# Weights of a held group released at k = 5, 6, 7 in place of 1, 3, 5, and x tiles transposed 20 tiles after silu in place of 14

## Chip, cores and metric

One core of a Trainium2 chip runs the whole program. The metric is device time in microseconds, the median of several runs. TensorE is called PE here, VectorE DVE, ScalarE ACT, GpSimd POOL and SyncE SP.

## What is computed

Four transformer-like layers over a sequence of 512 tokens of width 1024, batch 1, in float32: two layers of a first block, then two of a second.

```python
def hybrid_layer(x, ...):                       # first block, twice
    h = rms_norm(x, attn_pre_gain)
    u = h @ w_in                                # queries, keys, values, gates of two attentions
    o_a = swa_sink_attention(qa, ka, va, attn_sinks)
    o_b = nsa_attention(qb_raw, qb_rot, kc, vc, ks, vs, kw, vw, gates)
    mixed = sigmoid(g_a) * (o_a @ w_branch_a) + sigmoid(g_b) * (o_b @ w_branch_b)
    x = x + rms_norm(mixed @ w_out, attn_post_gain)
    h = rms_norm(x, ffn_pre_gain)
    return x + rms_norm(conv_ffn(h, ffn_w_up, ffn_conv_w, ffn_conv_b, ffn_w_down), ffn_post_gain)

    # second block, twice
    proj = rms_norm_2(x, norm1_w[i]) @ w_in[i]  # z, xbc, dt, q, k, v
    xbc = silu(depthwise_conv_centered(xbc, conv_w[i], conv_b[i]))   # 7 taps
    y_ssm = rms_norm_2((ssd(xs, dt, bm, cm) both ways + d_skip * xs) * silu(z), ssm_norm_w[i])
    x = x + concat(y_ssm, windowed_gqa(q, k, v, sink, band_bias)) @ w_out[i]
    g, u = split(rms_norm_2(x, norm2_w[i]) @ w_up[i])
    x = x + (silu(conv(g)) * u) @ w_down[i]
```

## The kernel before

Activations stand transposed: a tile is 128 features by 512 tokens, and the width is eight such tiles. All dense products go through one stream of weights, `Stream` (`W`): 3680 tiles of 128 x 128, packed in the order of their use into 460 chunks of `CH` = 8 tiles. A product in float32 precision is three matmuls (`mm3`, lines 530 to 532): high weights by high activations, low weights by high, high by low. High and low parts are float32r tiles.

A chunk passes through three steps. `load` has SP fetch it into one of four buffers `wraw` (line 306). `conv` makes its two parts, in one of four buffers each. For most chunks ACT writes the negated weights, rounded to float32r, to `wl` (line 319), then POOL issues a DMA that adds the exact weights from DRAM onto them (line 320), which leaves the rounding error, and ACT writes the rounded weights to `wh` (line 324). For chunks in the middle of an FFN DVE makes `wl` by a subtraction instead (line 329). `release(c)` is the step that drives both: it loads up to chunk c + 7 and converts up to chunk c + 4, so the conversion goes into the buffers of chunk c. As a rule `W.next` calls it when the stream enters a new chunk. The program is scheduled by hand (`manual_schedule`): each engine works through its instructions in the order in which the Python code issues them, and a wait holds up all that is behind it on that engine.

`W.defer(n, fn)` runs `fn` when the stream has gone n weight tiles further; that is the clock by which small work is placed between the matmuls.

A seam joins two dense stages around an rms norm. The last tiles of the first stage are made in two halves of 256 tokens (`HA`, `HB`), so that the norm of the first half can run while the second is being multiplied. `halves` goes over the eight tiles; in each step DVE scales and adds (lines 1445, 1447), ACT and DVE make `h` and `hl` (`split`, lines 420 and 421), and for the second half ACT also squares `x` and issues a store of it, `xd` (line 1455). What is left of these steps is in a generator, `hs.rest`.

`dense_group` makes four output tiles at once over the eight input tiles. Where `hs.rest` is there it goes over its weights twice: a first round over k = 0 to 7 on the first half of the tokens and a second on the other half. After each k of either round it takes one step of `hs.rest`; the last `h` tile's step is issued after k = 4 of the second round. Its 32 weight tiles are four chunks, c0 to c0 + 3, which fill all the buffers; `W.holding` keeps `W.next` from releasing any, and the second round does it by hand. This branch runs four times: for `ffn_w_up` and for the next layer's `w_in` (or `w_in_2`), in both layers of the first block. The groups start at chunks 49, 115, 164 and 230. The norm's sum is taken three tiles after the group and `finish`, which evacuates the four accumulators, runs seven tiles after it.

In the second block `layer2` makes eight x tiles of the conv (`conv_evac` at names x0 to x7), with tiles of q between the first five. An evacuation multiplies by the norm; then ACT and POOL start the seven-tap sum, DVE adds the other five taps (line 1582), and seven tiles later ACT applies silu (line 1587). `then` is `x_tokens` (or `b_tokens` for B0 and B1): four PE transposes into `xtp` (line 1697) and four ACT copies to `xtok` (line 1699). After the eighth x tile the z tiles follow, and between them the backward states (`advance`, line 1783 and 1787), whose product is read at `yo` (line 1869). All tiles of 128 x 512 come from one pool of 66 slots.

Of the kernel before, what the change touches and what calls it, by code (L numbers as in the profile page):

```python
# [249 lines left out]
def trunk_kernel(ctx: ExitStack, tc: tile.TileContext, xT, positions, wts, cst_d, oh_d, rb_d, cw1_d,  # L250
# [14 lines left out]
    def big(name, dt=F32):  # L265
        return pools["t"].tile([128, T], dt, tag="t", name=name)
# [7 lines left out]
    def bank(name, hold=False):  # L274
        b = banks.pop(0)
        t = psum.tile([128, T], F32, tag=f"b{b}", name=name)
        if hold:
            held[id(t)] = (b, t)
        else:
            banks.append(b)  # L280
        return t

    def free(t):
        banks.append(held.pop(id(t))[0])
# [4 lines left out]
    class Stream:  # L289
# [56 lines left out]
        def next(self, key):  # L346
            self.due(self.t)
            c, i = divmod(self.t, CH)
            if i == 0 and not self.holding:
                self.release(c - 1)  # L350
            name, l, r, cols = PLAN[self.t]
            assert (name, l, r) == key[:3], (PLAN[self.t], key)
            self.t += 1
            h, lo = self.hl[c]
            s = slice(128 * i, 128 * i + 128)
            return h[:, s], lo[:, s]
# [15 lines left out]
    W = Stream()  # L372
# [88 lines left out]
    def rstd_a(sq, n, act=False):  # L461

        sq.sums(len(sq.p))
        ps = sq.stat
        v = small(4, "var")
        V.tensor_reduce(v, ps[:, 0:128 * len(sq.p)].rearrange("p (a j) -> p j a", j=128)[:, 0:4, :], AX.X, OP.add)
        free(ps)
        r4 = small(4, "rs")
        if act:
            A.activation(v, v, AF.Sqrt, bias=epst, scale=1.0 / n)  # L470
            V.reciprocal(r4, v)
            return r4
        t4 = small(4, "rt")
        V.tensor_scalar(v, v, 1.0 / n, EPS, op0=OP.mult, op1=OP.add)
        V.tensor_scalar(r4.bitcast(I32), v.bitcast(I32), -0.5, float(0x5F3759DF), op0=OP.mult, op1=OP.add)
        for _ in range(3):
            V.tensor_mul(t4, r4, r4)
            V.scalar_tensor_tensor(t4, t4, -0.5, v, op0=OP.mult, op1=OP.mult)
            V.scalar_tensor_tensor(r4, t4, 1.5, r4, op0=OP.add, op1=OP.mult)
        return r4  # L480
# [18 lines left out]
    def rstd_b(r4, name="R"):  # L499
        R = big(name)  # L500
        pb = spread(r4)
        V.tensor_copy(R, pb)
        free(pb)
        return R
# [4 lines left out]
    class Tiles(list):  # L509
# [6 lines left out]
        def then(self, f):  # L516

            if self.rest is None:
                f()
            else:  # L520
                self.due.append(f)
# [3 lines left out]
    def mm3(acc, w, x, first, last, cs=None):  # L525
        wh, wl = w
        xh, xl = x
        if cs is not None:
            acc, xh, xl = acc[:, cs], xh[:, cs], xl[:, cs]
        PE.matmul(acc, wh, xh, start=first, stop=False)  # L530
        PE.matmul(acc, wl, xh, start=False, stop=False)  # L531
        PE.matmul(acc, wh, xl, start=False, stop=last)  # L532
# [28 lines left out]
    def dense_group(keys, hs, evacs, sq, store, x=None, after=None):  # L561

        accs = [bank("acc", True) for _ in range(4)]
        n = KT
        r4 = []
        if hs.rest is None:
            for k in range(n):
                for acc in accs:  # L570
                    mm3(acc, W.next(keys(k)), hs[k], k == 0, k == n - 1)
                if x is not None and k < 4:
                    sq.add(x[2 * k])
                    sq.add(x[2 * k + 1])
            r4.append(rstd_a(sq, D))
        else:
            c0 = W.t // CH
            ws = {}
            for k in range(n):
                for a, acc in enumerate(accs):  # L580
                    ws[k, a] = W.next(keys(k))
                    W.holding = True
                    mm3(acc, ws[k, a], hs[k], k == 0, k == n - 1, HA)
                next(hs.rest, None)
            for k in range(n):
                for a, acc in enumerate(accs):
                    mm3(acc, ws.pop((k, a)), hs[k], k == 0, k == n - 1, HB)
                next(hs.rest, None)
                if k % 2 and k < n - 1:
                    W.release(c0 + k // 2)  # L590
            run(hs.rest)
            hs.rest = None
            W.holding = False
            for f in hs.due:
                f()
            W.defer(3, lambda: r4.append(rstd_a(sq, D)))

        def finish():
            store["R"] = rstd_b(r4[0])
            late = [ev(acc) for acc, ev in zip(accs, evacs)]  # L600
            for acc in accs:
                free(acc)
            for f in late:
                if f:
                    f()
            if after:
                after()
        W.defer(5 if r4 else 7, finish)

    def run(gen):  # L610
        for _ in gen:
            pass
# [236 lines left out]
    def layer1(l, x, hs, sq, gnext, side):  # L849
# [186 lines left out]
        def after():  # L1036
            W.drip(rt)
            cw[0], cw[1] = windows(st.pop("kcb")), windows(st.pop("vcb"))
            for nm in ("ka", "qa0"):
                sw[nm] = swap(st[nm])  # L1040

        dense_group(win, hs, [evac_r(nm) for nm in ("kcb", "vcb", "ka", "qa0")], sq, st, x, after)
        x = None
        for j in range(1, 4):
# [260 lines left out]
        def pair(i):  # L1305
            if l == 0 and i > 2:
                side.step(1)
            if i == 0:
                dense_group(key("ffn_w_up", l), hs, [conv(0, "a0"), conv(FT, "v0"), conv(1, "a1"),
                                                     conv(FT + 1, "v1")],  # L1310
                            sq3, st3, x)
                x.clear()
            elif i > 1:
                run(dense(key("ffn_w_up", l), hs, conv(i, f"a{i}")))
                run(dense(key("ffn_w_up", l), hs, conv(FT + i, f"v{i}")))
            later(i, gated)
# [235 lines left out]
    def layer2(l, x, hs, sq, gnext):  # L1552
# [13 lines left out]
        def conv_evac(idx, name, wait=1, then=None):  # L1566
            def f(acc):
                u = big("u")
                V.tensor_mul(u, acc, st["R"])

                def late():
                    c = big("c")
                    A.activation(c, u, AF.Identity, bias=cb[:, idx:idx + 1], scale=cw[:, 36 + idx:37 + idx])
                    t = big("ct")
                    A.activation(t, u, AF.Copy, scale=cw[:, idx:idx + 1])
                    G.tensor_add(c[:, 3:T], c[:, 3:T], t[:, 0:T - 3])  # L1576

                    def taps():
                        for k in (1, 2, 4, 5, 6):
                            d = k - 3  # L1580
                            lo, hi = max(0, -d), min(T, T - d)
                            V.scalar_tensor_tensor(c[:, lo:hi], u[:, lo + d:hi + d],  # L1582
                                                   cw[:, 12 * k + idx:12 * k + idx + 1], c[:, lo:hi], op0=OP.mult,
                                                   op1=OP.add)

                        def silu():
                            A.activation(c, c, AF.Silu)
                            st[name] = c
                            if then:
                                W.defer(14, lambda: then(c))  # L1590
                        W.defer(7, silu)
                    W.defer(wait, taps)
                return late
            return f

        def raw_evac(name, scale=None):
# [7 lines left out]
            return f  # L1604

        dense_group(win, hs, [conv_evac(m, nm, w, th) for m, nm, w, th in (
            (8, "B0", 5, lambda c: b_tokens(0, c)), (9, "B1", 21, lambda c: b_tokens(1, c)),
            (10, "C0", 37, None), (11, "C1", 53, None))], sq, st, None if l else x)
# [590 lines left out]
```

## Time and profile before

| | |
|---|---|
| Median of 3 timed runs | 3111.31 us (3110.29 to 3114.95) |
| Profiled execution, its own time | 3115.91 us |
| Its span, first to last instruction | 3114.1 us |
| Mean granted clock of PE | 0.989 |
| PE, DVE, ACT, POOL busy | 97%, 62%, 54%, 15% |
| HBM read, written | 402.45 MB, 21.10 MB |
| Mean of the DMA engines over the span | 140 GB/s |

Times in rows are microseconds from the span's start. A row of the timeline gives the start, the duration, the engine and the source line, the operation, the tiles written and read, and in brackets how long the engine had been idle before it and what ended that. Where an engine name has a q (SPq, ACTq), its queue only issued a DMA. The granted clock is 1.0 for 2.4 GHz and 0.5 for 1.2 GHz.

### The profile page before, as it was taken

To read this page: it belongs to the slowest core of one execution; us is meant where nothing else is said; L and a number is where in the kernel's file an instruction comes from. 1 tells how busy PE (TensorE), PEld (TensorE's weight loads), DVE (VectorE), ACT (ScalarE), POOL (GpSimd) and SP (SyncE) were. 2 spreads that over 40 slices of the span, in tenths; PEclk is the share of its full clock that TensorE was granted. 3 is DMA by queue.
4 is the path that set the end of the run, shared out by engine and by line. 5 is a ranking of instruction groups with operands and counts; after the bars stand their busy time and mean duration, and the time that the engine had idled before them with its cause. 6 is when DMAs were issued, how large, how long until landed. Compare 5 with 4: busy or idle time off the path is not lost.

```text
span 3114.1 us, 41037 instructions
## 1 busy us (share of the span) xinstructions
PE 3034.8 (97%) x15024; PEld 2523.0 (81%) x15024; DVE 1917.4 (62%) x3726; ACT 1670.8 (54%) x3014; POOL 482.4 (15%) x482
## 2 busy tenths in 40 slices
PE   9999999999999999999999989999999998999998
PEld 8778888888877888888876778888888676888887
DVE  7677477374677738737576686463546768646353
ACT  4568554343457855434467777432346777743232
POOL 1222200000222210000025422000002542200000
PEclk9999999999999999999999999999999999999999
DMA  7744759475764385333577745633357874563432
GB/s 234 175 109 92 187 139 136 107 118 163 197 169 109 83 202 137 107 95 112 144 174 212 184 106 118 164 108 121 98 157 165 216 183 96 122 166 102 128 96 68
DMA packets 143270, 435.68 MB, mean 140 GB/s; under 512 B 17083, under 2 KB 22459, under 8 KB 143068
## 3 DMA queue, kind: packets, MB, share of 16 engines
q1 hardware_dynamic: 106396, 309.83, 33.2%
q0 software_dynamic: 32064, 114.83, 21.7%
q10 hardware_dynamic: 4608, 8.39, 0.7%
q8 instruction: 119, 1.95, 0.3%
q14 instruction: 83, 0.68, 0.1%
HBM read 402.45 MB, written 21.10 MB: 136 GB/s over the span
## 4 chain that ended last, share of the span: by engine, by line
PE 76%; ACT 8%; issue 7%; DVE 6%; DMA 2%; POOL 2%; SPq 0%; ACTq 0%; DVEq 0%; POOLq 0%
PE acc L530 22%; PE acc L532 22%; PE acc L531 22%; PE ops L757 2%; PE pt L739 2%; ACT wl L319 1%; DMA wl<-in_wts 1%; ACT p L2126 1%; PE sp L712 1%; DVE c L1582 1%; PE sp L713 1%; DVE X L692 1%; ACT pth L745 1%; POOL c L1576 1%; ACT of L767 1%
## 5 line engine op out<-in xcount | busy, mean ns | idle before, releaser
L530 PE MATMUL acc<-h,wh 128*128 128x512 f32 (+1 forms) x2592 | 1014.3, 391 | 9.0 <-ACT h L420 4.6
L531 PE MATMUL acc<-h,wl 128*128 128x512 f32 (+1 forms) x2592 | 987.4, 381 | 4.0 <-DMA wl<-in_wts 3.9
L532 PE MATMUL acc<-hl,wh 128*128 128x512 f32 (+1 forms) x2592 | 987.8, 381 | 0.6 <-DVE hl L421 0.4
L530 PEld LDWEIGHTS acc<-h,wh 128*128 128x128 f32 x2592 | 491.1, 189 | 101.5 <-issue 8.0
L532 PEld LDWEIGHTS acc<-hl,wh 128*128 128x128 f32 x2592 | 490.1, 189 | 96.4 <-DVE hl L421 1.9
L531 PEld LDWEIGHTS acc<-h,wl 128*128 128x128 f32 x2592 | 491.3, 190 | 91.8 <-DMA wl<-in_wts 5.6
L324 ACT ACTIVATE wh<-wraw 128x1024 fp32r<-128x1024 f32 x408 | 427.5, 1049 | 240.9 <-PE acc L532 205.7
L320 POOL DMA_DIRECT2D wl<-in_wts x216 | 188.1, 871 | 1943.3 <-ACT wl L319 1397.7
L329 DVE TENSOR_TENSOR wl<-wraw,wh 128x1024 fp32r<-128x1024 f32 x244 | 296.9, 1219 | 92.3 <-ACT wh L324 84.6
L530 PE MATMUL acc<-ah,wh 128*128 128x512 f32 (+1 forms) x726 | 278.2, 383 | 0.0
L319 ACT ACTIVATE wl<-wraw 128x1024 fp32r<-128x1024 f32 x216 | 226.8, 1050 | 95.2 <-PE acc L531 84.4
L532 PE MATMUL acc<-al,wh 128*128 128x512 f32 (+1 forms) x726 | 277.8, 383 | 0.0
L531 PE MATMUL acc<-ah,wl 128*128 128x512 f32 (+1 forms) x726 | 277.7, 383 | 0.0
L1293 ACT ACTIVATE c<-u,prm 128x512 f32<-128x512 f32 x88 | 71.1, 817 | 203.4 <-DVE u L1289 203.4
L739 PE MATMUL pt<-cst,p 128*128 128x128 f32 x752 | 145.4, 281 | 17.7 <-DVE nm L2124 4.2
L531 PEld LDWEIGHTS acc<-ah,wl 128*128 128x128 f32 x726 | 136.5, 188 | 26.7
L532 PEld LDWEIGHTS acc<-al,wh 128*128 128x128 f32 x726 | 136.4, 188 | 26.7
L530 PEld LDWEIGHTS acc<-ah,wh 128*128 128x128 f32 x726 | 136.5, 188 | 26.4
L1151 ACT ACTIVATE p<-p,nm 128x128 f32<-128x128 f32 x192 | 102.1, 532 | 62.6 <-DVE nm L1149 59.8
L745 ACT ACTIVATE pth<-pt 128x256 fp32r<-128x256 f32 (+2 forms) x320 | 130.7, 411 | 7.5 <-PE pt L739 5.1
L739 PEld LDWEIGHTS pt<-cst,p 128*128 128x128 f32 x752 | 93.8, 142 | 44.8 <-ACT p L2126 12.1
L1582 DVE SCALAR_TENSOR_TENSOR c<-u,prm,c 128x510 f32<-128x510 f32 (+2 forms) x120 | 98.5, 821 | 40.9 <-POOL c L1576 37.5
(339 smaller groups left out, 4809.9 us busy)
## 6 DMA issues: line engine op xcount, KB each, us to landing
wraw<-in_wts SPq DMA_DIRECT2D x460, 512.0 KB, 5.0
wl<-in_wts POOLq DMA_DIRECT2D x216, 512.0 KB, 7.1
cum<-cum_d SPq DMA_DIRECT2D x64, 256.0 KB, 7.2
xd<-x ACTq DMA_DIRECT2D x32, 256.0 KB, 2.0
x<-xd SPq DMA_DIRECT2D x32, 256.0 KB, 6.6
bias<-bias_d SPq DMA_DIRECT2D x32, 192.0 KB, 2.4
x<-in_xT SPq DMA_DIRECT2D x16, 256.0 KB, 8.0
cw<-in_cw SPq DMA_DIRECT2D x16, 256.0 KB, 7.2
```

What stands on the lines that cost most here:

```text
L319: A.activation(lo, r, AF.Copy, scale=-1.0)
L320: G.dma_start(out=lo, in_=wts[c], accum_op=OP.add)
L324: A.activation(h, r, AF.Copy)
L329: V.tensor_sub(lo, r, h.bitcast(F32))
L530: PE.matmul(acc, wh, xh, start=first, stop=False)
L531: PE.matmul(acc, wl, xh, start=False, stop=False)
L532: PE.matmul(acc, wh, xl, start=False, stop=last)
L739: PE.transpose(pt[:, 128 * n:128 * n + 128], t[:, 128 * (kb - b0):128 * (kb - b0) + 128], ident)
L745: A.activation(th[:, 0:w], pt[:, 0:w], AF.Copy)
L1151: A.activation(p[:, 0:w], p[:, 0:w], AF.Exp, bias=nm[:, col:col + 1], scale=-1.0, accum_out=den[:, col:col + 1])
L1293: A.activation(c, u, AF.Identity, bias=cb[:, idx:idx + 1], scale=cw[:, 88 + idx:89 + idx])
L1582: V.scalar_tensor_tensor(c[:, lo:hi], u[:, lo + d:hi + d], cw[:, 12 * k + idx:12 * k + idx + 1], c[:, lo:hi], op0=OP.mult, op1=OP.add)
```

## The change

It has two parts. In `dense_group`'s second round the three hand-made releases, of chunks c0, c0 + 1 and c0 + 2, are made after k = 5, 6 and 7 in place of k = 1, 3 and 5. In `conv_evac` the transposes of a conv tile are deferred by 20 weight tiles after silu in place of 14; that holds for B0, B1 and the eight x tiles of both layers of the second block.

```diff
@@ -586,8 +586,8 @@
                 for a, acc in enumerate(accs):
                     mm3(acc, ws.pop((k, a)), hs[k], k == 0, k == n - 1, HB)
                 next(hs.rest, None)
-                if k % 2 and k < n - 1:
-                    W.release(c0 + k // 2)
+                if k >= n - 3:
+                    W.release(c0 + k - (n - 3))
             run(hs.rest)
             hs.rest = None
             W.holding = False
@@ -1587,7 +1587,7 @@
                             A.activation(c, c, AF.Silu)
                             st[name] = c
                             if then:
-                                W.defer(14, lambda: then(c))
+                                W.defer(20, lambda: then(c))
                         W.defer(7, silu)
                     W.defer(wait, taps)
                 return late
```

## Rows read from the trace of the kernel before

**Rows 1.** Head of the page: busy time of each engine.

```profile
PE 3034.8 (97%) x15024; PEld 2523.0 (81%) x15024; DVE 1917.4 (62%) x3726; ACT 1670.8 (54%) x3014; POOL 482.4 (15%) x482
```

**Rows 2.** PE's waits: what waited for what: us in total, times, longest.

```profile
PE acc L531 <- DMA wl<-in_wts: 3.9, 4, 1.4
PE hid L935 <- issue: 3.7, 2, 2.5
PE xtp L1697 <- ACT c L1587: 2.8, 1, 2.8
```

**Rows 3.** Windows (us; busy by engine; PEclk; DMA): first group's second round.

```profile
414.87:426.39 11.52, 11.52 (x98) 11.52 (x97) 8.13 (x19) 10.85 (x17) 2.38 (x3) 1.00 0.80 225
```

**Rows 4.** Timeline of ACT, first group's second round.

```profile
415.31 0.51 ACT L420 ACTIVATE h<-x,prm 128x256 fp32r<-128x256 f32 x1 [0.21 <-DVE x L1447]
...
416.56 0.51 ACT L420 ACTIVATE h<-x,prm 128x256 fp32r<-128x256 f32 x1 [0.21 <-DVE x L1447]
...
417.83 1.06 ACT L319 ACTIVATE wl<-wraw 128x1024 fp32r<-128x1024 f32 x1 [0.24 <-PE acc L531]
...
423.48 0.50 ACT L420 ACTIVATE h<-x,prm 128x256 fp32r<-128x256 f32 x1
...
424.40 1.04 ACT L319 ACTIVATE wl<-wraw 128x1024 fp32r<-128x1024 f32 x1
```

**Rows 5.** Timeline of POOL, then of PE, around the first group's end.

```profile
419.19 0.86 POOL L320 DMA_DIRECT2D wl<-in_wts  x1 [14.86 <-ACT wl L319]
...
426.67 0.50 PE L531 MATMUL acc<-h,wl 128*128 128x512 f32 x1
...
427.23 0.40 PE L530 MATMUL acc<-h,wh 128*128 128x512 f32 x1
...
427.93 0.39 PE L530 MATMUL acc<-h,wh 128*128 128x512 f32 x1
```

**Rows 6.** DMA issues (KB, us to landing) around 419, 790, 891 and 810.

```profile
wl<-in_wts POOLq DMA_DIRECT2D x1, 512.0 KB, 7.4
...
wl<-in_wts POOLq DMA_DIRECT2D x1, 512.0 KB, 8.8
...
wl<-in_wts POOLq DMA_DIRECT2D x1, 512.0 KB, 5.2
...
t<-kcb SPq DMA_DIRECT2D x2, 128.0 KB, 10.1
```

**Rows 7.** Timeline of ACT, second rounds of the second and fourth group.

```profile
787.21 0.51 ACT L420 ACTIVATE h<-x,prm 128x256 fp32r<-128x256 f32 x1 [0.21 <-DVE x L1447]
...
789.41 1.06 ACT L319 ACTIVATE wl<-wraw 128x1024 fp32r<-128x1024 f32 x1 [1.18 <-PE acc L531]
...
1554.60 0.51 ACT L420 ACTIVATE h<-x,prm 128x256 fp32r<-128x256 f32 x1 [0.21 <-DVE x L1447]
...
1555.54 1.04 ACT L319 ACTIVATE wl<-wraw 128x1024 fp32r<-128x1024 f32 x1
```

**Rows 8.** Timeline of PE at three waits in the second block.

```profile
1631.26 0.88 PE L1697 MATMUL xtp<-cst,c 128*128 128x128 f32 x4 [2.77 <-ACT c L1587]
...
1689.50 1.18 PE L1869 MATMUL yo<-state,c 128*128 128x512 f32 x1 [4.03 <-ACT state L1783]
...
2465.87 1.22 PE L1869 MATMUL yo<-state,c 128*128 128x512 f32 x1 [4.05 <-ACT state L1783]
```

**Rows 9.** Windows behind three of PE's waits, columns as in rows 3.

```profile
1631.50:1634.90 3.40, 3.40 (x11) 2.74 (x10) 2.17 (x7) 2.73 (x4) 0.89 (x1) 0.51 0.80 154
822.60:829.40 6.80, 6.80 (x23) 5.74 (x22) 3.41 (x8) 2.67 (x4) 3.43 (x4) 0.50 0.51 98
...
797.97:812.00 14.03, 12.74 (x63) 10.41 (x62) 8.14 (x22) 4.17 (x5) 1.93 (x3) 1.00 1.06 288
```

**Rows 10.** Timeline of ACT, x stage's end in the second block's first layer.

```profile
1664.41 0.75 ACT L1699 ACTIVATE xtok<-xtp 128x128 f32<-128x128 f32 x4
1667.81 0.63 ACT L1743 ACTIVATE zt<-z 128x512 f32<-128x512 f32 x1 [2.65 <-DVE z L1741]
```

## The prediction, made before the changed kernel was run

> **What bounds the kernel now.** I read the head of the page first: TensorE (PE) is busy 3034.8 of 3114.1 us [rows 1]. So a change can win only from the roughly 80 us in which PE stands still or runs at half clock, and it loses wherever it makes PE wait for something that is only just in time today. The profiled execution took 3115.91 us by its own time (span 3114.1 of it), 4.6 above the median of the three timed runs, 3111.31. Everything below is a difference, so I apply the sum to either.
>
> Second view, PE's waits [rows 2]. Two of them touch the change. The wait of the low weight matmul for `wl`, from the accumulating DMA, is 3.9 us in 4 places. The wait of the x transposes for ACT's silu is 2.8 us in one place. The reader should also note what isn't there: no wait for late `h` tiles inside a group's second round. I checked that in the stretches from the first to the last matmul of a second round: PE is busy 11.52 of 11.52 us in the first group, at full clock [rows 3]; the other three look the same. (The trace has more waits for `h`, but at the start of a first round.)
>
> The branch of `dense_group` that is changed runs four times: at the FFN and at the next layer's input, in each of the two layers of the first block. I call its chunks c0 to c0+3, and c0+4 the one that PE takes first after the round.
>
> **Part 1: the release moves from k = 1, 3, 5 to k = 5, 6, 7.** No instruction is added or removed. A release issues one raw load on SP and the conversion of one chunk: ACT writes `wl` = -raw, POOL issues the accumulating DMA onto it, ACT writes `wh`. Today c0+4's pair stands in ACT's queue between the halves of `h` tile 4 and tile 5, and c0+5's between tiles 6 and 7. Moved behind k = 5, all of it stands behind `h` tile 7 and its square.
>
> What this removes: about 4 us of ACT work ahead of tiles 5 to 7, which then come up to 3 us sooner. It is worth nothing, since PE doesn't wait for those tiles [rows 3].
>
> What it costs: c0+4's `wl` starts later. In the first group `h` tiles come every 415.31 to 416.56 = 1.25 us when nothing stands between [rows 4]. Tile 4 starts at 416.56, so tile 7 can start at 416.56 + 3 x 1.25 = 420.31, and ACT is through with it and its square 0.92 us later (423.48 to 424.40 today [rows 4]): 421.2. Today `wl` starts at 417.83. The delay is 3.4 us. POOL's issue follows `wl`'s start by 419.19 - 417.83 = 1.36 us [rows 5] and the DMA lands 7.4 us after its issue [rows 6], so today at 426.6, and PE's first matmul with c0+4's low part starts at 426.67 [rows 5]. There is no slack at all: in the first group the 3.4 us go straight to PE. In the second group tile 4 starts at 787.21 and `wl` at 789.41 [rows 7], where ACT had waited 1.18 us for PE: 787.21 + 3.75 + 0.92 = 791.88, a delay of 2.5. In the fourth, 1554.60 + 4.67 = 1559.27 against 1555.54 [rows 7]: 3.7. The third is the first in the next layer and gets 3.4. Sum 13.0 us of new PE idle time, on top of what groups two and four wait there already: 14.03 - 12.74 = 1.3 us behind the second [rows 9] and 1.4, the longest of [rows 2], behind the fourth. Bounds: the DMA may land 1 us sooner, as the stores of `xd` are then nearly done, or 1.4 us later, since the three conversions, each two ACT operations of about 1 us [rows 4], follow each other at once and crowd the queues (8.8 us from issue to landing in the second group against 7.4 in the first [rows 6]); -4 to +6 over four groups. c0+5 and c0+6 come later too, but are wanted 8 and 16 tiles of 427.93 - 427.23 = 0.7 us later [rows 5], and are covered by that.
>
> One rule speaks against this sum. The trace's transfers take 7.4 and 8.8 us here, and the quickest of the run's 216 took 5.2 [rows 6]. The Trainium skill, "DMA: Bandwidth & Descriptors", section on the anatomy of one SWDGE DMA, fits 2.0 us plus the bytes over 436 KB per us, an estimate of 3.2 us for these 512 KB; by it c0+4 would land at 425.8 in the first group and nothing would be lost. The rows speak against it, as none of these transfers came near it; the rival below prices it from the rows.
>
> To the idle time comes the clock. After the 2.77 us idle before the x transposes [rows 8] PE ran 3.4 us at a granted 0.51, and after the 2.5 us wait at `hid` it ran 6.8 us at 0.50 [rows 9]: 1.2 in place of 2.4 GHz, so 1.7 and 3.4 us lost. The wait of 1.3 us for `wl` behind the second group left the clock up: 797.97 to 812 stands at 1.00 [rows 9]. With 3.4 to 5.1 us idle I expect the low clock in all four places, at 1.7 to 3.4 us each; I take 2.5, so 10 us (bounds 6.8 and 13.6).
>
> Given back: after the second group PE waits 2.5 us at `hid` [rows 2], for tiles that come by copies `t<-kcb` taking 10.1 us to land [rows 6], on queues still full of the weight loads of the group's end. PE will come there some 5 us later while those loads end about as early as before plus 2.5 us, so the wait shrinks, and with it its 3.4 us of low clock: up to 5.9. I take 4 (bounds 0 and 5.9). The other three groups have no such wait behind them that I can name.
>
> Queues that are passed: on SP the raw loads of c0+8 and c0+9 wait for the ACT conversions and move back by up to 3 us; behind them stand the loads of parameters and `cw`, wanted much later. On POOL nothing stands near. On DVE only the sums of squares move, to an earlier time; they are wanted only three tiles after the group, so I cost that at nothing.
>
> Part 1: 13.0 + 10 - 4 = +19.
>
> **Part 2: `then` at 20 tiles in place of 14.** It moves four PE transposes and four ACT copies for each x tile (and four and one for B0, B1). At 1631.26 PE has waited 2.77 us for silu of x tile 3 [rows 8]; six tiles are some 4 us, so the transposes come after silu, and the wait goes, with its 1.7 us of low clock: -4.5. Is it lost at the next wait? In the first layer of this block, which has that stall, PE waits 4.03 us for `state` at 1689.50; in the second, which hasn't, 4.05 us at 2465.87 [rows 8]. The chain before that wait starts from PE's own output, so the gain stays. But x tile 5's four copies (0.75 us at 1664.41) lie today ahead of a 2.65 us pause of ACT; moved on by six tiles they fall into the stretch from 1667.81 [rows 10], where ACT works without a pause up to `state`. That is 0.75 us for each layer, +1.5. Part 2: -3.0 (bounds -4.5 and 0). Tiles x5 and x6 live six tiles longer in the pool of 66 slots; I cost it at nothing, as `z` tiles are then only beginning to fill it.
>
> Sum: +19 - 3.0 = +16 us, 3127 at the median (3132 for the profiled execution). PE stays the bound; what is late after the change is c0+4's `wl`.
>
> **The rivals.** (a) *The transfer is hidden anyway*: c0+4's `wl` lands about 4 us after issue, so PE finds it ready in all four groups. Price: the waits of 3.9 us go, part 2 gives 3.0, so -7: 3104, faster. It decides from 4 us on. Against it: 216 transfers, quickest 5.2 us [rows 6]. Chance 0.04. The fit that the Trainium skill gives on its DMA page, above, is the one rule for it.
> (b) *The idle time doesn't lower the clock.* +13.0 - 4 - 3.0 = +6, 3117, at the edge of what can be told from no change. For it: waits up to 1.4 us leave it up. Against it: 2.5 and 2.77 us didn't [rows 9]. Chance 0.17.
> (c) *The crowded queues*: three accumulating DMAs and three raw loads within 6 us; every landing is 1.4 us later and the low clock lasts longer: 16 + 6 + 3.6 = +26, 3137. For it: 8.8 us where more loads run [rows 6]. Chance 0.17.
> (d) *Part 2 gives nothing*, because the wait for silu follows the shift or returns at `state`: 3130. Chance 0.07.
> My forecast has the rest, 0.55.
>
> **How the numbers follow.** Range: from (b) with a good landing, 3115, to a little over (c), 3140; outside it (a) and tails. About 0.2% or 6 us is what a measurement of this kernel tells from no change. Faster by more: (a), 0.04. Within: half of (b) and small tails, 0.13. Slower: 0.83.
>
> **What would show it.** Right: in each of the four groups ACT's `L319` for c0+4 stands directly behind the last `L420` and square, 2.5 to 3.7 us later than now, and PE's waits for `wl` grow from 3.9 to about 17 us in 4 places, each followed by a stretch of low clock; the wait at `xtp` is gone, `state` stands at 4.0 to 4.8 twice; `hid` waits less in the second layer. Wrong: PE waiting for `h` inside a second round today (then it would gain); `wl` landing within 5 us of its issue; full clock after the idle; or a new wait for a pool slot in the x stage.

## The result, and the profile after

The changed kernel takes 3132.58 us (median of 4 runs, 3131.91 to 3134.42) against 3112.81 for the kernel before in the same comparison (4 runs, 3110.29 to 3114.95). The ratio is 1.0063, with a 95% interval from 1.0051 to 1.0076, so it is slower by 16 to 24 us. The profiled execution took 3132.55 us by its own time, 16.6 more than the 3115.91 of before.

The account starts at the head of the page of after, the line that answers to [rows 1] (busy us of each engine, share of the span, instructions):

```profile
span 3130.8 us, 41040 instructions
...
PE 3036.3 (97%) x15024; PEld 2522.9 (81%) x15024; DVE 1919.4 (61%) x3726; ACT 1671.4 (53%) x3014; POOL 486.1 (16%) x482
```

PE's busy time is 1.5 us longer than in [rows 1], the span 16.7. Span less busy time, PE's idle time, has thus gone from 79.3 to 94.5 us: in these two profiles nearly all of the loss is waiting. What low clock adds in the other runs is taken up with the prediction, below. PE's waits of after (what waited for what: us in total, times, longest):

```profile
PE acc L531 <- DMA wl<-in_wts: 17.9, 8, 3.6
PE yo L1869 <- ACT state L1783: 9.4, 2, 4.7
...
PE yo L1869 <- DVE state L1787: 4.1, 4, 1.6
...
PE hid L935 <- issue: 1.2, 1, 1.2
```

Against [rows 2] the wait for `wl` grew from 3.9 to 17.9 us, `hid` (a small product in the first block's attention, made from what the copies `t<-kcb` bring) fell from 3.7 to 1.2, and the x transposes' wait for `c` is no longer there. The wait for `state` grew from 4.03 and 4.05 [rows 8] to 9.4 in two. The wait for DVE's part of `state` is 4.1 us; its row in before is

```profile
PE yo L1869 <- DVE state L1787: 2.5, 4, 0.7
```

ACT's timeline in the first group's second round (start, duration, line, operation, idle before) shows the mechanism of part 1; it answers to [rows 4]:

```profile
420.60 0.51 ACT L420 ACTIVATE h<-x,prm 128x256 fp32r<-128x256 f32 x1 [0.21 <-DVE x L1447]
...
421.01 0.62 ACT L434 ACTIVATE sq<-x 128x512 f32<-128x512 f32 x1
421.54 1.05 ACT L319 ACTIVATE wl<-wraw 128x1024 fp32r<-128x1024 f32 x1
422.48 1.05 ACT L324 ACTIVATE wh<-wraw 128x1024 fp32r<-128x1024 f32 x1
```

The first conversion now stands behind the last `h` tile and its square. POOL's issue follows, the transfer flies for some 7 us, and PE stands at the first low matmul of c0+4. The next lines are from after: POOL's issue, its row among the DMA issues (KB, us to landing) in the first and in the fourth group, and PE's four waits behind the four groups, from PE's timeline:

```profile
422.87 0.86 POOL L320 DMA_DIRECT2D wl<-in_wts  x1 [18.25 <-ACT wl L319]
...
wl<-in_wts POOLq DMA_DIRECT2D x1, 512.0 KB, 7.0
...
wl<-in_wts POOLq DMA_DIRECT2D x1, 512.0 KB, 7.7
```

```profile
429.97 0.70 PE L531 MATMUL acc<-h,wl 128*128 128x512 f32 x1 [3.22 <-DMA wl<-in_wts]
...
803.43 0.80 PE L531 MATMUL acc<-h,wl 128*128 128x512 f32 x1 [3.64 <-DMA wl<-in_wts]
...
1202.46 0.50 PE L531 MATMUL acc<-h,wl 128*128 128x512 f32 x1 [2.77 <-DMA wl<-in_wts]
...
1574.70 0.80 PE L531 MATMUL acc<-h,wl 128*128 128x512 f32 x1 [3.64 <-DMA wl<-in_wts]
```

Together 13.27 us. Behind the second and fourth group 1.29 and 1.44 were there before, so the change added 10.5 us here. The two other waits of [rows 2] lie elsewhere, ahead of the second rounds (0.47 us at 412.01, 0.70 at 1181.88). The rest of the 17.9 is one wait of 3.55 us in the x stage, shown below, and three small ones.

The windows behind these waits, columns as in [rows 3] (the clock is the last but two):

```profile
430.10:433.50 3.40, 3.40 (x9) 2.63 (x10) 0.00 (x0) 0.00 (x0) 0.00 (x0) 0.50 1.06 280
803.40:812.40 9.00, 8.97 (x25) 7.46 (x26) 1.96 (x12) 0.00 (x0) 0.00 (x0) 0.50 1.06 251
1202.50:1212.00 9.50, 9.50 (x48) 7.96 (x49) 5.23 (x18) 1.85 (x3) 0.00 (x0) 1.00 0.76 201
1574.70:1583.80 9.10, 9.10 (x25) 7.49 (x26) 1.98 (x12) 0.00 (x0) 0.00 (x0) 0.50 1.06 261
1647.00:1657.00 10.00, 10.00 (x51) 8.41 (x52) 5.03 (x8) 6.69 (x13) 2.83 (x3) 1.00 0.88 210
```

The reader should see that three of the four waits are followed by a granted 0.50, the 1.2 GHz level, and that two of those stretches last 9 us and more where [rows 9] showed 3.4 and 6.8. The 2.77 us behind the third group and the 3.55 us in the x stage left the clock at 1.00.

Last, the x stage of after, where part 2 was to save 3 us (timelines of DVE, ACT, POOL and PE):

```profile
1629.86 0.23 DVE L1630 TENSOR_SCALAR dtr<-dte 128x128 f32<-128x128 f32 x1 [3.15 <-ACT dte L1626]
...
1636.56 0.68 DVE L1569 TENSOR_TENSOR u<-acc,R 128x512 f32<-128x512 f32 x1
1637.28 0.81 ACT L1573 ACTIVATE c<-u,prm 128x512 f32<-128x512 f32 x1 [6.67 <-DVE u L1569]
1638.61 1.04 ACT L319 ACTIVATE wl<-wraw 128x1024 fp32r<-128x1024 f32 x1
1638.79 1.09 POOL L1576 TENSOR_TENSOR c<-c,ct 128x509 f32<-128x509 f32 x1 [10.37 <-ACT ct L1575]
1639.96 0.87 POOL L320 DMA_DIRECT2D wl<-in_wts  x1
1646.96 0.50 PE L531 MATMUL acc<-h,wl 128*128 128x512 f32 x1 [3.55 <-DMA wl<-in_wts]
```

The wait for `c` is gone, and 3.55 us for a weight chunk have come in its place. The chunk's conversion stands in ACT's queue behind `c` of an x tile, that behind DVE's `u`, and that behind a DVE which stood 3.15 us waiting for ACT's `dte` (the Exp in `dt_all`, the chain of small operations that makes dt; called the dt path here). ACT came to that Exp at 1629.52, behind the two operations of a weight conversion (from 1626.21) and a table load of 1.28 us. In the kernel before the same chain is there, and the two waits of ACT and DVE are about as long:

```profile
1616.52 0.23 DVE L1630 TENSOR_SCALAR dtr<-dte 128x128 f32<-128x128 f32 x1 [3.16 <-ACT dte L1626]
...
1623.95 0.81 ACT L1573 ACTIVATE c<-u,prm 128x512 f32<-128x512 f32 x1 [7.34 <-DVE u L1569]
...
1626.62 0.87 POOL L320 DMA_DIRECT2D wl<-in_wts  x1
...
1634.92 0.42 PE L531 MATMUL acc<-h,wl 128*128 128x512 f32 x1
```

There the chunk landed 7.0 us after its issue, at 1633.6, and PE came for it at 1634.92, after 2.77 us of waiting and 1.7 us of low clock. Without these PE would have come at 1634.92 - 2.77 - 1.7 = 1630.45, and would have stood 1633.6 - 1630.45 = 3.2 us. That sum could be made from the trace of before.

### The profile page after: what moved, and what is told of

It is laid out like the page before. It is cut to its first block, busy times and chain, and to the rows that moved or that the text cites. A ratio compares the mean times of both kernels' runs of the same rounds, so it can differ in the third digit from the quotient of the medians.

```text
span 3130.8 us, 41040 instructions
## 1 busy us (share of the span) xinstructions
PE 3036.3 (97%) x15024; PEld 2522.9 (81%) x15024; DVE 1919.4 (61%) x3726; ACT 1671.4 (53%) x3014; POOL 486.1 (16%) x482
## 4 chain that ended last, share of the span: by engine, by line
PE 52%; ACT 6%; issue 6%; DVE 5%; POOL 2%; DMA 1%; SPq 0%; DVEq 0%; POOLq 0%; ACTq 0%
PE acc L530 15%; PE acc L531 15%; PE acc L532 15%; PE pt L739 1%; PE ops L757 1%; ACT p L2126 1%; ACT wl L319 1%; DVE c L1582 1%; POOL c L1576 1%; ACT pth L745 1%; ACT of L767 1%; PE sp L712 1%; DVE X L692 1%; PE sp L713 1%; DVE p L2124 1%
## 5 line engine op out<-in xcount | busy, mean ns | idle before, releaser
L531 PE MATMUL acc<-h,wl 128*128 128x512 f32 (+1 forms) x2592 | 989.3, 382 | 17.9 <-DMA wl<-in_wts 17.9
L531 PEld LDWEIGHTS acc<-h,wl 128*128 128x128 f32 x2592 | 491.5, 190 | 106.9 <-DMA wl<-in_wts 20.7
L531 PE MATMUL acc<-ah,wl 128*128 128x512 f32 (+1 forms) x726 | 277.7, 383 | 0.0
L739 PE MATMUL pt<-cst,p 128*128 128x128 f32 x752 | 145.4, 280 | 19.8 <-ACT p L1151 4.5
L531 PEld LDWEIGHTS acc<-ah,wl 128*128 128x128 f32 x726 | 136.5, 188 | 26.6
```

The lines of the kernel that those rows point to most:

```text
L739: PE.transpose(pt[:, 128 * n:128 * n + 128], t[:, 128 * (kb - b0):128 * (kb - b0) + 128], ident)
```

## The experiments

The theory after the result: (T1) the loss is part 1 alone, and in it one thing, the landing of c0+4's low half; the later release of c0+5 and c0+6 and the freed `h` tiles 5 to 7 count for nothing. (T2) part 2 gains nothing, because the wait for `c` and the late weight chunk have a common cause, DVE's stand for the Exp. Rivals: that the crowding of three conversions and three accumulating transfers in a row costs the time, whichever comes first; that the loss is in both parts; and that part 2 pays or costs only by x5's copies ahead of `state`.

Times in the table are medians in us and ratios to the kernel before run on the same chip (3112.37, median of 29 runs, for the first four; 3113.86, of 33, for the others).

| run | time | ratio, 95% interval |
|---|---|---|
| part1_alone | 3130.63 (5 runs) | 1.0060, 1.0046 to 1.0073 |
| part2_alone | 3113.64 (12) | 1.0005, 0.9995 to 1.0015 |
| first_chunk_early | 3113.58 (11) | 1.0002, 0.9992 to 1.0011 |
| part1_low_by_dve | 3112.17 (11) | 1.0000, 0.9991 to 1.0008 |
| first_chunk_mid | 3122.16 (11) | 1.0026, 1.0017 to 1.0035 |
| part2_five_tiles | 3112.64 (10) | 0.9992, 0.9983 to 1.0002 |
| dt_spread | 3109.26 (11) | 0.9987, 0.9978 to 0.9995 |
| dve_first_and_dt | 3108.65 (11) | 0.9981, 0.9972 to 0.9990 |

**part1_alone** makes the first edit of the change and leaves `then` at 14.

```diff
-                if k % 2 and k < n - 1:
-                    W.release(c0 + k // 2)
+                if k >= n - 3:
+                    W.release(c0 + k - (n - 3))
```

> Part 1 alone (releases after k = 5, 6, 7; x tiles at 14 as before). The theory that the first released chunk's low half comes too late: about 2 to 3.5 us of PE idle behind each of the four groups, with low clock behind some of them, less what is given back at hid; in the changed kernel's trace the four groups together lost about 13 us, so 3126 here (3123 to 3131), with PE's waits for wl at 13 to 15 us in 4 main places and the wait of 2.8 us at xtp still there. The rival that the late release is harmless and the loss comes from part 2: within 3 us of the kernel before.

Measured: 0.60% slower, 18.7 us, at the upper end of what was expected; these runs can't tell it from the loss of the whole change. Its page's head, its PE waits, and the window behind its third group, where PE had waited 3.63 us:

```profile
PE 3043.4 (97%) x15024; PEld 2529.8 (81%) x15024; DVE 1918.4 (61%) x3726; ACT 1671.7 (53%) x3014; POOL 487.5 (16%) x482
...
PE acc L531 <- DMA wl<-in_wts: 13.0, 5, 3.6
...
PE xtp L1697 <- ACT c L1587: 2.7, 1, 2.7
...
1200.40:1209.90 9.50, 9.49 (x26) 7.82 (x27) 1.96 (x12) 0.00 (x0) 0.00 (x0) 0.50 0.75 197
```

Part 1 is the loss. The waits behind its four groups are 2.95, 3.32, 3.63 and 2.86 us, and here all four are followed by a granted 0.50, for 3.3, 9.1, 9.5 and 6.8 us. With a span of 3131.4, idle time is 8.7 us up against before and busy time 8.6.

**part2_alone** sets `then` to 20 tiles and keeps the old releases.

```diff
-                                W.defer(14, lambda: then(c))
+                                W.defer(20, lambda: then(c))
```

> Part 2 alone (x tiles at 20, releases after k = 1, 3, 5 as before). My forecast was -3 us. The theory after seeing the changed kernel's trace, that the wait at xtp is replaced by one for a chunk's low half 13 us further on and that both waits for state grow: PE's wait at xtp gone, one wait of about 3.5 us for wl in the first layer of the second block, waits at yo larger by about 1.5 us in each layer; total +1 to +4. The rival that the forecast stands and the changed kernel's new wl wait is a follow-up of part 1: -3, no wl wait there.

Measured: no difference that these runs can tell; the interval is -1.6 to +4.7 us. Its PE waits, and PE's row in the x stage:

```profile
PE yo L1869 <- ACT state L1783: 9.4, 2, 4.7
PE acc L531 <- DMA wl<-in_wts: 6.9, 5, 3.9
...
1627.82 0.50 PE L531 MATMUL acc<-h,wl 128*128 128x512 f32 x1 [3.91 <-DMA wl<-in_wts]
```

The wait for `c` is gone and one of 3.91 us for `wl` has taken its place, with the releases as they were: the new wait belongs to part 2, not to part 1. ACT's `state` grew from 8.1 to 9.4 us in the two layers together, about half of what was expected at `yo`, and DVE's `state` not at all: 2.5 us as before.

**first_chunk_early** releases c0+4 at k = 1 as before, and c0+5 and c0+6 at k = 6 and 7 as after.

```diff
-                if k % 2 and k < n - 1:
-                    W.release(c0 + k // 2)
+                if k in (1, n - 2, n - 1):
+                    W.release(c0 + (1, n - 2, n - 1).index(k))
```

> Releases after k = 1, 6, 7: only the first released chunk is freed as early as before, the other two are as late as in the change or nearly so; x tiles at 14. The theory that the first chunk alone decides: within 1 us of the kernel before, PE's waits for wl near 3.9 us. The rival that later releases crowd the transfers, or that all three chunks are late: half or more of part 1's loss stays, +6 us or more, with waits for wl one and two chunks behind the group.

Measured: no difference, 1.0002. The wait for `wl` is back to

```profile
PE acc L531 <- DMA wl<-in_wts: 3.3, 5, 1.3
```

So the late release of two of the three chunks costs nothing that these runs can tell, and neither does the ACT work behind the round. All of the loss hangs on the first chunk.

**part1_low_by_dve** keeps all three late releases, but lets DVE make the low half of c0+4 by a subtraction, so that neither POOL's issue nor the transfer lies on the chain.

```diff
+HEAD = (53, 119, 168, 234)
+for _c in HEAD:
+    BYV[_c] = True
...
-            while len(self.subs) > (1 if later and BYV[self.conved - 1] else 0):
+            while len(self.subs) > (1 if later and BYV[self.conved - 1] and self.conved - 1 not in HEAD else 0):
```

> Part 1 (releases after k = 5, 6, 7; x tiles at 14), and the low half of the first chunk behind each group is made by DVE as wraw minus wh, which takes 1.2 us, in place of ACT's copy, POOL's issue and the accumulating DMA. The theory that the landing of that DMA is what PE waits for: the waits for wl behind the four groups are gone or under 1 us each, the low clock there too, and the time is at or a little below the kernel before, 3107 to 3114. The rival that the late place in ACT's queue alone costs it, whatever follows: a loss of 5 us or more stays.

Measured: 1.0000. DVE's subtraction and PE's first low matmul of c0+4 in the first group (three lines were added above, so L534 is L531):

```profile
426.41 1.22 DVE L332 TENSOR_TENSOR wl<-wraw,wh 128x1024 fp32r<-128x1024 f32 x1
...
427.69 0.50 PE L534 MATMUL acc<-h,wl 128*128 128x512 f32 x1 [0.45 <-DVE wl L332]
```

The release is as late as in the changed kernel, and 0.45 us are left of the 3.22; behind the third and fourth group it is 0.65 and 0.82, behind the second none. What costs is the late release together with the time from the conversion to the landing, 8.3 us by way of POOL in the first group (421.54 to 422.87 + 7.0). By way of DVE, from ACT's `wh` to the end of the subtraction, it is 5.6 us (422.07 to 426.41 + 1.22), and with the same release the loss is gone.

**first_chunk_mid** releases the three chunks at k = 3, 5 and 6, between the two kernels.

```diff
-                if k % 2 and k < n - 1:
-                    W.release(c0 + k // 2)
+                if k in (3, 5, 6):
+                    W.release(c0 + (3, 5, 6).index(k))
```

> Releases after k = 3, 5, 6; x tiles at 14. The first chunk's conversion stands behind h tile 6, so its low half starts about 2.2, 1.2, 1.8 and 2.5 us later than before in the four groups, against 3.4, 2.5, 3.1 and 3.7 in the change. The theory that each us of delay goes straight to PE: waits for wl of some 2.2, 2.5, 1.9 and 3.9 us, 10.5 in all, and a time between the kernel before and part 1 alone, 3118 to 3124, the rest over the added 7 us being low clock. The rival that there is slack of some 2 us, or that low clock alone makes the loss: within 3 us of before.

Measured: 0.26% slower, 8.1 us, a little under half of part 1. The waits for `wl`:

```profile
PE acc L531 <- DMA wl<-in_wts: 9.6, 5, 2.9
```

Behind the four groups they are 1.36, 2.83, 1.89 and 2.86 us, 8.9 in all where 10.5 were expected. Over the three places of the release that were run the loss grows with the delay of the first chunk, as a late landing would have it.

**part2_five_tiles** moves `then` to 20 for x0 to x4 alone, so that the copies of x5 (and of x6, x7, B0 and B1) stay where they were.

```diff
-                                W.defer(14, lambda: then(c))
+                                W.defer(20 if name in ("x0", "x1", "x2", "x3", "x4") else 14, lambda: then(c))
```

> x tiles x0 to x4 at 20, x5 to x7 and B0, B1 at 14; releases as before. The theory that part 2 has two separate effects, the wait at xtp replaced by one for wl (x3) and four more ACT copies before state (x5): the wait of 3.5 to 3.9 us for wl in the first layer of the second block is there, xtp's gone, and the waits at yo are 4.0 and 0.7 us in both layers as in the kernel before, not 4.7 and 1.4; time within 3 us of before. The rival that the waits at yo grow because PE comes earlier or another tile's copies moved: 4.7 us stays.

Measured: 0.9992, no difference that these runs can tell, at the edge of one. Its PE waits, and PE's row in the x stage:

```profile
PE yo L1869 <- ACT state L1783: 8.1, 2, 4.0
PE acc L531 <- DMA wl<-in_wts: 7.2, 5, 3.3
...
PE yo L1869 <- DVE state L1787: 3.2, 4, 1.4
...
1625.48 0.50 PE L531 MATMUL acc<-h,wl 128*128 128x512 f32 x1 [3.27 <-DMA wl<-in_wts]
```

The wait for ACT's `state` is back at 8.1 us, so the copies of the tiles left alone are what lengthened it. ACT's rows in the first layer say which: between ACT's pause ahead of `zt` and its `state` after has three sets of `xtok` copies (1685.25, 1691.38 and 1692.52) and before has two (1671.24 and 1677.37), x5's standing ahead of the pause [rows 10]. The exchange of the `c` wait for a `wl` wait stays. The wait for DVE's `state` is 3.2 us, between the 2.5 of before and the 4.1 of after: x5's copies don't explain all of that one, and part2_alone, where they move, shows 2.5.

**dt_spread** is the kernel before, with the dt path's work on DVE held back by seven more turns of the scheduler behind the Exps, so that DVE doesn't stand for them.

```diff
-            yield
+            for _ in range(8):
+                yield
```

> The kernel before, with seven more weight tiles between the exponentials of dt_all and DVE's first use of them. The theory that both waits, the one at xtp before and the one for wl after part 2, have one cause, DVE standing 3.2 us for ACT's exponential in dt_all with the x taps behind it, and ACT's conversions behind those: the wait at xtp shrinks to under 1 us without a new one for wl, 3 to 5 us less by the trace of the x stage of the first layer. The rival that DVE simply has too much work there: a wait of 2 us or more stays at xtp or comes at wl.

Measured: 0.13% faster than before, 1.6 to 6.9 us by the interval. DVE in the x stage, and two of PE's waits (one line was added above):

```profile
1614.54 0.68 DVE L1569 TENSOR_TENSOR u<-acc,R 128x512 f32<-128x512 f32 x1
...
1621.70 0.22 DVE L1631 TENSOR_SCALAR dtr<-dte 128x128 f32<-128x128 f32 x1
...
PE acc L531 <- DMA wl<-in_wts: 2.8, 3, 1.2
...
PE xtp L1698 <- ACT c L1587: 0.5, 1, 0.5
```

DVE no longer stands for the Exp: `u` starts at 1614.54, where its row in before stands at 1623.23, 8.7 us sooner, of which 2.6 are the lead that this run has at the x transposes just ahead (1614.42 against 1616.97). The wait for `c` is 0.5 us where it was 2.77, and no wait for `wl` of over 1.2 us has come in its place. So the common cause of the two waits is the dt path ahead of the x taps in DVE's queue. T2 named the stand for the Exp alone; that isn't shown. The 6.1 us that are left of the 8.7 are the stand, 3.2, and 2.9 us of the dt path's own work on DVE, which has moved behind the taps as well (L1631 at 1621.70), and no run parts the two.

**dve_first_and_dt** puts together what had helped: c0+4 at k = 1, c0+5 and c0+6 late, its low half by DVE, and the held back dt path.

```diff
+HEAD = (53, 119, 168, 234)
...
+                if k in (1, n - 2, n - 1):
+                    W.release(c0 + (1, n - 2, n - 1).index(k))
...
+            for _ in range(8):
+                yield
```

> Releases after k = 1, 6, 7 with the first chunk's low half made by DVE, x tiles at 14, dt_all spread as in dt_spread: all the causes named so far taken away. If each is a wait of PE by itself: 3.9 us of wl waits behind the groups and 4.4 us in the x stage go, 3104 to 3108, faster than both kernels. The rival that the waits behind the groups move on to the next one (hid in the second layer): -4 us or less, within the noise of before.

Measured: 0.19% faster than before, 3.1 to 8.7 us by the interval, a little less than expected (3108.65 against 3104 to 3108), and faster than the changed kernel by more than 20. Its PE waits:

```profile
PE hid L938 <- issue: 6.3, 2, 5.1
...
PE acc L534 <- DMA wl<-in_wts: 0.8, 2, 0.4
...
PE xtp L1701 <- ACT c L1590: 0.6, 1, 0.6
```

The waits for `wl` and `c` are nearly gone, but `hid` grew from 3.7 to 6.3 us. In the second layer PE comes to it 6.8 us sooner than in before (at 815.84 - 5.14 = 810.70 against 819.96 - 2.49 = 817.47), and the wait ends only 4.1 us sooner, as the `t<-kcb` copies take 11.3 us to land where [rows 6] has 10.1. So part of the time taken out ahead of `hid` is waited for there, which was the rival. The 0.6 us that the run has over dt_spread alone are less than can be told.

## Why the prediction was right, and which steps were not

Its total held: 16 us were forecast, the timed runs give 19.8 and the profiled execution 16.6. That the 16.6 comes so close is luck, as the profiled execution of before was 3.1 us above the median of its comparison (3115.91 against 3112.81). The mechanism of part 1 was the one that it named. The steps:

- **The 80 us to win from**: misread. 3114.1 - 3034.8 is the time in which PE stands still; the half clock lies in the busy time, and at a mean clock of 0.989 it costs an estimated 34 us more. No term of the sum rests on this.
- **Nothing is gained inside the second round**: right. No wait for `h` there was removed, and first_chunk_early, which also takes most of that ACT work out of the round, gains nothing.
- **The delay of c0+4**: right in kind, a little large. Idle time of 3.4, 3.8, 3.4 and 5.1 us was forecast behind the four groups, with what was there; it is 3.22, 3.64, 2.77 and 3.64. The term that was mis-sized is the flight, from POOL's issue to the landing: the sum kept that of before, 7.4, 8.8, 7.7 and 8.6 us in the four groups, and after has 7.0, 7.1, 7.1 and 7.7, 3.6 us less in all, close to the -4 of the bounds. Against PE's coming POOL's issue is later by 3.6, 4.1, 3.2 and 3.1 us, 14.0 where the sum had 13.0. The second group's 3.64 for 3.8 is luck: its delay is 1.6 us more than forecast, and its flight 1.8 less. 10.5 us were added where the sum had 13.0.
- **Flight**: 7.0 to 7.7 us. The Trainium skill, "DMA: Bandwidth & Descriptors", section on the anatomy of one SWDGE DMA, would give an estimate of 3.2 us for such a transfer; none of the four came near it, so the measurement decides, and with it rival (a) falls.
- **Crowded queues**, rival (c): wrong for the chunk that counts. With three conversions back to back the first chunk's transfer flew for a shorter time than before. Those behind it flew longer, in the first group 9.1 and 11.0 us where before has 7.9 and 8.9, but PE didn't wait for them.
- **Low clock**: right in three of four places, in part1_alone in all four. The stretches in after add to at least 3.4 + 9.0 + 9.1 = 21.5 us, half of which is lost, 10.7; those in part1_alone to 28.7, so 14.4, more than the bound of 13.6. The sum had 10. Rival (b), full clock after the idle time, holds for the third group only. But the stretches are longer and fewer than the sum had them.
- **Low clock over the whole run**: about as large as the sum had it, by an estimate. PE's busy time in the profiles doesn't show 10 us: it rose by 1.5 us in after and by 8.6 in part1_alone. Low stretches that before has in places the change doesn't touch, of 6.8 us at 51.20 and 6.6 at 771.50, are missing from after. From single profiles the term is known only to within several us. The mean granted clocks of the timed runs tell more: 0.985 to 0.988 in the four runs of after, 0.9868 on average, and 0.9897 on average over the 62 runs of before in the experiments. If PE was the limit throughout, low clock costs 41 us of after and 32 of before, an estimate of 9 more; among the 62 runs a clock lower by 0.001 goes with a time longer by some 2.2 us, which makes it 6. The sum had some 6 as well, 10 less what it gave back at `hid` and at the x transposes.
- **Given back at `hid`**: right, and more than forecast. Its wait in the second layer is gone in after and in part1_alone, with the 3.4 us of low clock, 5.9 us in all where 4 were taken. The copies `t<-kcb` landed in 4.2 us, where [rows 6] had 10.1.
- **Part 2, -3.0**: wrong. "The transposes come after silu, and the wait goes" held; the step that failed is "so the gain stays". I compared the wait for `state` in the two layers, and found that it would not take the gain; I didn't ask what PE would need next. That was a weight chunk, 3.7 us behind the transposes in before (1634.92), with 1.3 us to spare. Rival (d) had the wait follow or return at `state`; it returned at `wl`, in a place that it didn't name. part2_alone gives about 0 (-1.6 to +4.7 us).
- **x5's copies ahead of `state`**: right. 4.7 us against 4.03, and 4.0 again where x5 isn't moved.
- **DVE's `state`**: not forecast. It costs 1.6 us more in after. In part2_alone, with the same shift, the total is 2.5 as before; in part2_five_tiles it is 3.2 and in dt_spread, where `then` isn't moved, 3.5. So it doesn't follow x5's copies, and its cause stays open.

Part 1 alone was put at 19 and measures 18.7, in part by luck. By the terms of its own profile it is 12.76 - 2.73 = 10.0 of idle time, 14.4 of low clock and 5.9 given back, 18.5: less idle time and more given back than forecast, made up for by more low clock. In the same way the 17.9 us that PE waits for `wl` in after meet the forecast's "about 17 us in 4 places" only by the 3.55 of the x stage; the four places hold 13.3. That the sum fell short of the timed 19.8 by 3.8 us is part 2's 3.0 that wasn't there, and a remainder smaller than the interval.

## What to carry to other kernels

When a buffer is freed later, follow the whole way of the first thing that needs it, here conversion, POOL's issue and landing, down to the instruction that wants it: with no slack there, every us of delay is idle time, and the engine that is unburdened doesn't count. When a wait is taken away, ask what the engine wants next and when that lands, and trace both back to see whether they wait for the same thing; if they do, mend that thing, and not the order at the wait. Two chunks of three could be freed late for nothing: only the first one had a date.

## What the runs showed of the hardware

The low clock doesn't follow from the length of the wait alone. In the second and the fourth group PE waits 1.69 us for `h` as the group begins, in before as in after. The windows behind these waits in before, then in after:

```profile
771.50:778.10 6.60, 6.60 (x31) 6.60 (x32) 4.48 (x14) 3.62 (x7) 0.86 (x1) 0.50 0.86 189
1541.00:1548.00 7.00, 7.00 (x61) 7.00 (x60) 6.79 (x21) 3.82 (x8) 0.87 (x1) 1.00 0.78 184
```

```profile
775.50:785.00 9.50, 9.29 (x79) 9.16 (x77) 8.46 (x23) 5.58 (x10) 0.86 (x1) 1.00 0.72 171
1546.40:1549.70 3.30, 3.30 (x17) 3.30 (x17) 2.42 (x9) 2.27 (x5) 0.86 (x1) 0.50 0.64 144
```

The same wait was followed by 1.2 GHz in the second group of before and in the fourth of after, and by full clock in the two others. In the same way 2.77 us behind the third group left the clock up in after, and 2.77 us at the x transposes in before didn't [rows 9]. In single profiles of kernels that differ by nothing in PE's work before the x stage, such stretches come and go; one of 6.6 us, as in the first row, costs 3.3 us. That is as much as part 2 was forecast to give, so an edit of that size can be judged by timed runs alone and not by the spans of two profiles. What decides whether the clock falls in one place and not in another stays open.
